# RWKV inverse on compact 64x64 blocks in quarters of TensorE's array, fold products alternating over the heads

## Chip, cores, metric

The kernel runs on one core of a Trainium2 chip. The metric is the device time of one execution in microseconds; of several executions the median is taken. Engines are named as in the profile: PE is TensorE, PEld its weight loads, DVE VectorE, ACT ScalarE, POOL GpSimd, SP the engine that issues most DMAs.

## What is computed

Two blocks of a language model, in float32, on 512 tokens of 1024 channels. The first block mixes the tokens with eight heads of forgetting attention and eight heads of an RWKV-7 recurrence, projects the result, and ends with a gated feed-forward layer. The second has an HGRN2 and a retention mixer and a retrieval over 16384 experts. The change lies in the RWKV recurrence alone. Cut to that, the reference is:

```python
def rwkv7_scan(r, w, k, v, a, b):
    """S_t = S diag(w_t) + (S a_t) b_t^T + v_t k_t^T ;  y_t = S_t r_t."""
    def step(S, inp):
        r_t, w_t, k_t, v_t, a_t, b_t = inp
        Sa = jnp.einsum('bhij,bhj->bhi', S, a_t)
        S = S * w_t[:, :, None, :] + Sa[..., None] * b_t[:, :, None, :] + v_t[..., None] * k_t[:, :, None, :]
        return S, jnp.einsum('bhij,bhj->bhi', S, r_t)
```

## The kernel before

The whole program is one list of instructions per engine. The kernel writes them in a loose order, and a scheduler at build time fixes the order on each engine; the engines then run their lists strictly in order and wait for each other by semaphores. So a change of a few instructions also moves their neighbours.

The recurrence is done in chunks of 64 tokens. Two heads share the 128 partitions: the even head lies on partitions 0 to 63, the odd one on 64 to 127. There are four such pairs of heads (c = 0 to 3), each with eight chunks, which are worked on in two groups of four: eight groups u in all. Within a chunk the 64 steps are turned into products, for which the inverse of I - N is needed, N a strictly triangular 64x64 matrix of each head and chunk.

For each pair of heads `rwkv_elem` (L655) makes decay, keys and gates of 512 tokens: long operations on VectorE and ScalarE. For each group then:

- `rwkv_group` (L721) makes the operands: scaled keys and queries (bh, BK, AR), the score products `ge` (L767: K = 64 rows, one head's half of the array, one bank a head), and masks them into NT (N of four chunks, L772), GM and AR. In NT each chunk has 128x128 elements with the two heads' blocks on the diagonal and zeros elsewhere (a memset, L738).
- `rwkv_inv` (L791) doubles the inverse, for two chunks at a time; two such halves h = 0, 1 alternate, with a bank pair each (i0 in A, i1 in B). It starts from the identity with the first level masked in (Tt, L808 and L809), transposed to T (L807 and L812). For each of five levels it makes NT^T T (L804 into PSUM, copied to Y by ScalarE, L818), Tt^T Y (L804, masked into T by VectorE, L821), and, but for the last level, the transpose of T (L807), copied to Tt by ScalarE (L825). All products are 128x128 by 128x128; both heads are in one product, since the matrices are block-diagonal.
- `rwkv_fold` (L829) multiplies the inverse with GM (`wg`, L836, copied to GS by ScalarE, L838), then with AT (`wf`, L843, K = 64, four products of one head and then four of the other, each head into bank C, which has one buffer), and VectorE adds each result to M (L844).
- `rwkv_scan` (L846) goes through the four chunks in sequence: a product of state and values (`ys`, L862), whose result is copied back into SV by VectorE and ScalarE (L865, L866) before the next; then it normalises (L871 to L891).

The driver interleaves them as software stages: for each u it prepares group u + 2, inverts group u + 1, folds and scans group u (L1582 to L1586). Banks are given by a string, `RB = "acc ge wg; A i0; B i1; C pe gv wf ys; D gt ga lt"`, with two buffers each for acc, A and B, one each for C and D. Behind the stage comes the output projection: its first half, over the attention's results, does not depend on the recurrence and is placed by the scheduler into gaps of TensorE's list from 440 us on; all later parts follow it.

The inverse in the code, cut:

```python
# rwkv_inv, B = [128, 2, 128]
def product(out, a, b):
    nc.tensor.matmul(out, a, b, start=True, stop=True)
...
for m in (2, 4, 8, 16, 32):
    py = self.b(f"i{h}", B)
    each(product, py, nt, tf)
    y = self.S(B, name=f"Y{h}")
    nc.scalar.activation(y, py, AF.Copy)
    px = self.b(f"i{h}", B)
    each(product, px, tt, y)
    nc.vector.copy_predicated(tf, mask(self.lv, self.levT[m]), px)
```

Of the kernel before, what the change touches and what calls it, by code (L numbers as in the profile page):

```python
# [12 lines left out]
U32 = mybir.dt.uint32  # L13
AF = mybir.ActivationFunctionType
ALU = mybir.AluOpType
AX = mybir.AxisListType

T = 512
# [5 lines left out]
# ---------------------------------------------------------------- host layout  # L24
def fm_tiles(w, cols=None):
    """[K, N] -> one [128, (K/128)*128] block per 128 output columns, split into ring tiles of 1024."""
    w = w if cols is None else w[:, cols]
    k, n = w.shape
    a = w.reshape(k // 128, 128, n // 128, 128).transpose(2, 1, 0, 3)
    return a.reshape(n // 128, 128, k // 1024, 1024).transpose(0, 2, 1, 3).reshape(-1, 128, 1024)  # L30


def tm_tiles(w):
    """[K, N] -> ring tiles of [128, 2 k-chunks, 512 columns], column blocks outermost."""
    k, n = w.shape
    a = w.reshape(k // 256, 2, 128, n // 512, 512).transpose(3, 0, 2, 1, 4)
    return a.reshape(-1, 128, 1024)


def fmvec(v):  # L40
# [4 lines left out]
NDENSE = 3      # token tiles whose experts are all computed; the last tile gathers its experts' rows  # L45
NFIFO = 40
IN_ORDER = ((0, 0), (0, 1), (0, 2), (0, 3), (1, 0), (1, 1), (1, 2), (1, 3))      # projections: mixer, heads
ONEHOT = "DDPDDDPP"     # engine of the second one-hot, by quartet of a block
NEARLY, NLATE, NLAG = 25, 3, 10      # products with expert_u before and after the gate matrix
# [3 lines left out]
    [x for n in range(8) for x in [(1, n), (0, n + GATE_AHEAD)] if x[1] < 8]    # gate a, branch; block  # L53
ATTN_STEP = 2
ELEM_AT = 2
FB = "acc; A m fpt; B fs; C pe fpo0; D fpo1"      # banks of the mixers' products
RB = "acc ge wg; A i0; B i1; C pe gv wf ys; D gt ga lt"
# [3 lines left out]
def shape_consts():  # L61
# [12 lines left out]
    us = [lev(m) for m in (2, 4, 8, 16, 32)] + [lev(m).T for m in (1, 2, 4, 8, 16, 32, 64)]  # L74
    out["cu"] = np.concatenate(us, 1).astype(np.uint32)
    scm = np.ones((128, T), np.float32)
# [13 lines left out]
def prep(inp):  # L90
    """Lays the inputs out; every array is a permutation, slice or stack of inputs, or depends on shapes alone."""
# [77 lines left out]
# ---------------------------------------------------------------- program  # L169
class Prog:  # L170
# [14 lines left out]
    # storage: every name of a tile stands for a tag with its number of buffers in the pool of the phase  # L185
    def open(self, es, name, spec, right=True, psum=False):
        """spec: "tag buffers name name ...; ..." """
# [9 lines left out]
    def banks(self, spec):  # L197
        """spec: "bank name name; ..." """
# [24 lines left out]
    # ring of weight tiles  # L223
# [36 lines left out]
    # products  # L260
    def mm3(self, out, a, b, start, stop):
        """out += a^T b with a, b given as exact (hi, lo) parts"""
# [5 lines left out]
    def gemm_fm(self, X, M=128, bank="acc", parts=1):  # L268
        """one block of 128 output features x 512 tokens; X: list of (hi, lo) FM chunks"""
# [12 lines left out]
    def gemm_tm(self, X, banks=("A", "A", "B", "B"), done=None, tail=2, head=1, ps=None, stop=True, hold=0):  # L282
        """512 output columns x 4 token tiles; the tiles end one after the other,
        the end of a tile behind the norm of the one `hold` before it"""
# [27 lines left out]
    def split(self, src, name):  # L312
        """FM f32 chunk in SBUF -> exact parts"""
# [8 lines left out]
    # constants  # L322
    def consts(self):
# [8 lines left out]
        ld(self.cu, I["cu"].rearrange("p (m n) -> p m n", n=128)[:, 5:12])  # L332
# [4 lines left out]
        # derived per-channel vectors  # L337
# [13 lines left out]
        # lower bound: softmax over the two rows, first row  # L351
# [8 lines left out]
        # f = lb + (1 - lb) (tanh / 2 + 1/2) = tanh * c1 + c0  # L360
# [7 lines left out]
    def attn_consts(self):  # L368
        """constants of the first mixers only"""
# [7 lines left out]
        self.lv = self.b("lv", [128, 5, 128], U32)  # L377
        ld(self.lv, I["cu"].rearrange("p (m n) -> p m n", n=128)[:, 0:5])
# [9 lines left out]
    def first_loads(self):  # L388
        """tokens, the first gain and the first weights in the order of their use"""
# [29 lines left out]
    def rstd_of(self, ss, n, eps, w=1):  # L419
        """(ss / n + eps) ** -0.5 of a small tile"""  # L420
# [7 lines left out]
    def new_U(self):  # L428
        """8 FM chunks of exact parts"""
# [4 lines left out]
    def rstd_row(self, ss):  # L434
        """(sum + eps) ** -0.5 of the two scaled square sums of a row"""
# [6 lines left out]
    def square(self, x, ss):  # L442
        """sum of squares / D along the row"""
# [3 lines left out]
    def norm_tile(self, i, gb, banks=("C", "D"), ss=None):  # L447
        """rmsnorm of one token tile of self.X, into its columns of the FM chunks; ss: with its first square sum"""
# [24 lines left out]
    def norm_fm(self, gb):  # L473
        """rmsnorm of self.X as 8 FM chunks of exact parts"""
# [6 lines left out]
    def tm_norm(self, X, gp, gn, early=None):  # L481
        """self.X += rmsnorm(X^T w) * gp, and the FM chunks of rmsnorm(self.X) * gn;
        early: the two halves of the product begun with the first chunks"""
# [35 lines left out]
    # ------------------------------------------------------------ block 1  # L519
# [10 lines left out]
    def lat_part(self, U):  # L530
# [19 lines left out]
        # forget gates of the attention heads: rows 32..39  # L550
# [18 lines left out]
    def fox_proj(self, c, U):  # L569
        """queries, keys and values of two heads"""  # L570
# [84 lines left out]
    def rwkv_elem(self, c):  # L655
        """two heads of the RWKV group on 128 channels"""
# [5 lines left out]
        # decay  # L662
# [15 lines left out]
        # in-context rate  # L678
# [9 lines left out]
        # normalised key  # L688
# [16 lines left out]
        # gate and bonus  # L705
# [15 lines left out]
    def rwkv_group(self, c, g_, e):  # L721
        """operands of four chunks: with Z = [state; values] of a head and U = (I - N)^-1 A0^T Z,
        y = A1^T Z + B1^T U and the next state is D^T Z + Bu^T U"""
# [8 lines left out]
        ar = self.b("AR", [128, 4, 2, 2, 64])         # chunk, A0 or A1, head, token  # L732
# [938 lines left out]
```

## Time and profile before

| | us |
|---|---|
| median of 3 runs | 3137.03 |
| lowest, highest | 3127.26, 3152.71 |
| span of the profiled execution, first to last instruction | 3129.2 |

The page gives the span alone; the time of that execution beside it is not listed. A run's time takes in what lies around the span.

How to read the profile: the busy time of an engine is the union of its records. A matmul's record is modelled and includes the way through the array, so the next one starts before it ends, and gaps shorter than a record do not show. A float32 product appears as two records, each with a weight load, since it is done in two passes; a transpose as one. Shapes are written as rows of the array x columns of weights, then rows x moving columns, so `64*128 64x128` is a product that uses half of the rows. "Chain" is the sequence of work that ended last, followed back from the end.

### The profile page before, as it was taken

What the parts mean: (1) busy time and instruction counts of PE and PEld (TensorE: products, weight loads), DVE (VectorE), ACT (ScalarE), POOL (GpSimd) and SP (SyncE); (2) the same over time, 40 slices, a digit from 0 to 9 for tenths busy, and PEclk for the clock granted to TensorE, in tenths of its full rate; (3) what the DMA queues carried; (4) which work ended last, traced back from release to release, by engine and by line L of the source; (5) the groups of instructions that cost most, each with busy time, mean ns of one, the idle gap of its engine ahead of it and who ended that gap; (6) DMA issues with size and microseconds to landing.
All of it is one profiled execution on the core that took longest, in us unless ns stands there. A gap on an engine that the chain in (4) does not pass through costs nothing.

```text
span 3129.2 us, 40869 instructions
## 1 busy us (share of the span) xinstructions
PE 2961.4 (95%) x15129; PEld 2547.7 (81%) x15129; DVE 1938.7 (62%) x3421; ACT 1228.4 (39%) x1925; POOL 1508.5 (48%) x1150
## 2 busy tenths in 40 slices
PE   7999898999999999999999978888999999999998
PEld 6877787888878878888888868887888888888876
DVE  4247755443135653555423899997777777787788
ACT  5455644222243433444423324565333333333333
POOL 3222213222245652333323457866767677667665
PEclk9998999999999999999999989999999999999999
DMA  4120013333332213222333223446888988888886
GB/s 156 56 68 8 1 38 109 97 98 97 95 113 69 62 47 101 85 85 85 90 116 123 92 68 95 142 169 219 297 275 293 308 289 298 299 280 299 285 310 240
DMA packets 174359, 473.65 MB, mean 151 GB/s; under 512 B 15056, under 2 KB 64592, under 8 KB 172624
## 3 DMA queue, kind: packets, MB, share of 16 engines
q1 hardware_dynamic: 137296, 336.80, 33.8%
q0 software_dynamic: 36864, 134.23, 12.2%
q8 instruction: 120, 1.97, 0.3%
q14 instruction: 79, 0.65, 0.1%
HBM read 439.49 MB, written 31.46 MB: 151 GB/s over the span
## 4 chain that ended last, share of the span: by engine, by line
PE 69%; DVE 15%; DMA 7%; issue 5%; ACT 2%; POOL 1%; SPq 0%; DVEq 0%; POOLq 0%; ACTq 0%
PE acc L266 13%; PE acc L265 13%; PE acc L264 13%; DMA urow<-ev,ei 3%; PE A L266 3%; PE A L264 3%; PE A L265 3%; PE B L266 3%; PE B L265 3%; PE B L264 3%; DMA urow<-eu,ei 2%; PE pg L1377 2%; DVE lo L241 2%; PE i L804 1%; PE lev L981 1%
## 5 line engine op out<-in xcount | busy, mean ns | idle before, releaser
L241 POOL TENSOR_TENSOR lo<-raw,hi 128x1024 fp32r<-128x1024 f32 x278 | 689.6, 2481 | 912.9 <-ACT hi L238 875.8
L238 ACT ACTIVATE hi<-raw 128x1024 fp32r<-128x1024 f32 x501 | 529.3, 1057 | 1065.7 <-PE acc L265 441.4
L266 PE MATMUL acc<-u,lo 128*128 128x512 f32 (+3 forms) x2344 | 864.6, 369 | 39.2 <-DVE lo L241 21.2
L264 PE MATMUL acc<-u,hi 128*128 128x512 f32 (+3 forms) x2344 | 862.4, 369 | 15.0 <-ACT x L1392 6.3
L265 PE MATMUL acc<-u,hi 128*128 128x512 f32 (+3 forms) x2344 | 862.1, 368 | 0.7 <-DVE u L471 0.7
L266 PEld LDWEIGHTS acc<-u,lo 128*128 128x128 f32 (+1 forms) x2344 | 448.1, 191 | 96.2 <-DVE lo L241 27.6
L264 PEld LDWEIGHTS acc<-u,hi 128*128 128x128 f32 (+1 forms) x2344 | 447.8, 191 | 70.0 <-ACT eact L1392 6.7
L265 PEld LDWEIGHTS acc<-u,hi 128*128 128x128 f32 (+1 forms) x2344 | 448.3, 191 | 54.8 <-issue 2.7
L241 DVE TENSOR_TENSOR lo<-raw,hi 128x1024 fp32r<-128x1024 f32 x223 | 304.4, 1365 | 301.1 <-ACT hi L238 299.9
L1332 DVE SCALAR_TENSOR_TENSOR urow<-urow,h4row 128x1024 f32<-128x1024 f32 x128 | 201.5, 1595 | 109.2 <-DMA urow<-eu,ei 108.9
L1342 DVE SCALAR_TENSOR_TENSOR po<-urow,act,po 128x1024 f32<-128x1024 f32 x127 | 203.2, 1600 | 84.9 <-DMA urow<-ev,ei 83.5
L1324 POOL DMA_INDIRECT urow<-eu,ei x128 | 193.5, 1512 | 32.6 <-issue 19.0
L1324 POOL DMA_INDIRECT urow<-ev,ei x128 | 176.6, 1380 | 37.8 <-issue 18.2
L1403 ACT ACTIVATE wh<-wf 128x384 fp32r<-128x384 f32 x128 | 67.1, 525 | 272.3 <-PE D L265 243.5
L1368 DVE TENSOR_SCALAR ohA<-iota,slT 128x128 f32<-128x128 f32 x384 | 129.8, 404 | 0.9 <-PE pg L1377 0.7
L1377 PE MATMUL pg<-ohB,ohA 128*128 128x128 f32 x768 | 106.3, 280 | 25.0 <-DVE ohB L1374 12.5
L1377 PEld LDWEIGHTS pg<-ohB,ohA 128*128 128x128 f32 x768 | 97.4, 191 | 32.7 <-ACT gstage L1379 16.1
L1379 ACT ACTIVATE gstage<-pg 128x512 f32<-128x512 f32 x96 | 99.5, 1089 | 57.8 <-PE pg L1377 57.7
L1372 POOL TENSOR_SCALAR ohB<-iota,slT 128x128 f32<-128x128 f32 x144 | 98.2, 698 | 39.9 <-PE pg L1377 39.7
L266 PE MATMUL A<-hi,wl 128*128 128x512 f32 x256 | 95.8, 399 | 10.0 <-DVE wl L1404 9.9
L265 PE MATMUL A<-lo,wh 128*128 128x512 f32 x256 | 101.0, 395 | 0.8 <-POOL lo L241 0.8
L264 PE MATMUL A<-hi,wh 128*128 128x512 f32 x256 | 99.8, 390 | 0.6 <-ACT wh L1403 0.6
(539 smaller groups left out, 5395.9 us busy)
## 6 DMA issues: line engine op xcount, KB each, us to landing
raw<-ut SPq DMA_DIRECT2D x128, 512.0 KB
raw<-ev SPq DMA_DIRECT2D x128, 512.0 KB
raw<-w_ret SPq DMA_DIRECT2D x48, 512.0 KB
gd<-gstage SPq DMA_DIRECT2D x12, 2048.0 KB
gread<-gd SPq DMA_DIRECT2D x32, 768.0 KB
raw<-w_gu SPq DMA_DIRECT2D x44, 512.0 KB
raw<-w_hg SPq DMA_DIRECT2D x32, 512.0 KB
raw<-w_in SPq DMA_DIRECT2D x27, 512.0 KB
```

The lines of the kernel that those rows point to most:

```text
L238: self.nc.scalar.activation(hi, raw, AF.Copy)
L241: r = eng.tensor_tensor(lo, raw, hi.bitcast(F32), op=ALU.subtract)
L264: mm(out, a[0], b[0], start=start, stop=False)
L265: mm(out, a[0], b[1], start=False, stop=False)
L266: return mm(out, a[1], b[0], start=False, stop=stop).ins
L1324: r = nc.gpsimd.indirect_dma_start(out=u, out_offset=None, in_=src, in_offset=bass.IndirectOffsetOnAxis(ap=ei[:, s:s + 1], axis=0))
L1332: nc.vector.scalar_tensor_tensor(u, u, 1.0, row, op0=ALU.mult, op1=ALU.mult, accum_out=act[:, s:s + 1])
L1342: nc.vector.scalar_tensor_tensor(o, u, act[:, s:s + 1], o, op0=ALU.mult, op1=ALU.add)
L1368: nc.vector.tensor_scalar(A4[:, r], self.iota, sl[:, 0, k + r:k + r + 1], sl[:, 2, k + r:k + r + 1], op0=ALU.is_equal, op1=ALU.mult)
L1372: nc.gpsimd.tensor_scalar(B4[:, r], self.iota, sl[:, 1, k + r:k + r + 1], None, op0=ALU.is_equal)
L1377: last = nc.tensor.matmul(p[:, r, :], A4[:, r], B4[:, r], start=True, stop=True)
L1379: nc.scalar.activation(st[:, :, q * 4:q * 4 + 4].rearrange("p j t -> p t j"), p, AF.Copy)
```

## The change

The inverse keeps only the two heads' own 64x64 blocks, side by side on the partitions. NT, T, Tt and Y have 64 columns a chunk instead of 128, the memset of NT goes, and the masks become a table of their own (`cl`). A product of 128x128 becomes two of 64x64, on the upper left and on the lower right quarter of the array, and the transposes become plain products with a 64x64 identity (`ic`). The first product of the fold becomes two quarters as well; the second alternates over the heads, both results being held at once in the two buffers of acc. Line numbers of the new file are 1 to 6 away from those of the old one.

```diff
-RB = "acc ge wg; A i0; B i1; C pe gv wf ys; D gt ga lt"
+RB = "acc ge wg wf; A i0; B i1; C pe gv ys; D gt ga lt"
...
-    us = [lev(m) for m in (2, 4, 8, 16, 32)] + [lev(m).T for m in (1, 2, 4, 8, 16, 32, 64)]
+    us = [lev(m).T for m in (1, 2, 4, 8, 16, 32, 64)]
     out["cu"] = np.concatenate(us, 1).astype(np.uint32)
+    own = lambda a: np.concatenate([a[:64, :64], a[64:, 64:]], 0)
+    out["cl"] = np.concatenate([own(lev(m)) for m in (2, 4, 8, 16, 32)] + [own(lev(1).T)], 1).astype(np.uint32)
...
-        self.lv = self.b("lv", [128, 5, 128], U32)
+        self.lv = self.b("lv", [128, 6, 64], U32)
...
-        nt = self.S([128, 4, 128], name="NT")
+        nt = self.S([128, 4, 64], name="NT")
...
-        nc.gpsimd.memset(nt, 0.0)
...
-            TT(nt[R, :, 64 * par:64 * par + 64], pe[par][R, :, 0, :], mk[R, None, 0].to_broadcast(B3), op=ALU.mult)
+            TT(nt[R], pe[par][R, :, 0, :], mk[R, None, 0].to_broadcast(B3), op=ALU.mult)
...
     def rwkv_inv(self, e, g_, h):
-        B = [128, 2, 128]
+        HV = (slice(0, 64), slice(64, 128))
+        B = [128, 2, 64]
...
         def product(out, a, b):
-            nc.tensor.matmul(out, a, b, start=True, stop=True)
+            for i in range(2):
+                for R in HV:
+                    nc.tensor.matmul(out[R, i], a[R, i], b[R, i], start=True, stop=True)
         def transpose(out, a):
-            nc.tensor.transpose(out, a, self.ident)
-        nc.gpsimd.tensor_copy(tt, self.ident[:, None, :].to_broadcast(B))
-        nc.vector.copy_predicated(tt, mask(self.cu, self.levTt[1]), nt)
+            for i in range(2):
+                for R in HV:
+                    nc.tensor.matmul(out[R, i], a[R, i], self.ic[R], start=True, stop=True)
+        nc.gpsimd.tensor_copy(tt, self.ic[:, None, :].to_broadcast(B))
+        nc.vector.copy_predicated(tt, mask(5), nt)
...
     def rwkv_fold(self, e, g_):
...
         for i in range(4):
-            nc.tensor.matmul(pg[:, i, :], G["tf", i // 2][:, i % 2], G["gm"][:, i].rearrange("p a b -> p (a b)"), start=True, stop=True)
+            for R in HV:
+                nc.tensor.matmul(pg[R, i, :], G["tf", i // 2][R, i % 2], G["gm"][R, i].rearrange("p a b -> p (a b)"),
+                                 start=True, stop=True)
...
-        for par in range(2):
-            R = HV[par]
-            pf = self.b("wf", [128, 4, 2, 64])
-            for i in range(4):
-                nc.tensor.matmul(pf[:, i], G["at"][R, i, :], gs[R, i, :], start=True, stop=True)
-            nc.vector.tensor_tensor(G["m1"][:, :, par], pf, G["m1"][:, :, par], op=ALU.add)
+        pf = [self.b("wf", [128, 4, 2, 64]) for _ in range(2)]
+        for i in range(4):
+            for par in range(2):
+                R = HV[par]
+                nc.tensor.matmul(pf[par][:, i], G["at"][R, i, :], gs[R, i, :], start=True, stop=True)
+        for par in range(2):
+            nc.vector.tensor_tensor(G["m1"][:, :, par], pf[par], G["m1"][:, :, par], op=ALU.add)
```

The scheduler's order moves with it. The first place is TensorE's list in the middle of the stage, where an inverse runs beside the scan of the group before it. Before (a row is line, operation, result <- moving, weights or the other way round, size of the result, count; `i` are the banks of the inverse):

```order
L862 MATMUL ys<-SV,M_2306 128x64 x2
L804 MATMUL i_3061<-Y_3059,Tt_2935 128x128 x2
L807 MATMUL i_3198<-ident,Tt_3194 128x128 x2
L836 MATMUL wg<-GM,T_2928 128x128 x2
L804 MATMUL i_3202<-T_3187,NT 128x128 x2
L862 MATMUL ys<-SV,M_2306 128x64 x2
L804 MATMUL i_3215<-T_3195,NT 128x128 x2
```

After, in the same kind of place (L805 and L810 are the products and the former transposes of the inverse, L868 is `ys`):

```order
L868 MATMUL ys<-SV,M_2686 128x64 x2
L805 MATMUL i_3516<-Y_3514,Tt_3442 64x64 x4
L805 MATMUL i_3535<-Y_3533,Tt_3432 64x64 x4
L868 MATMUL ys<-SV,M_2686 128x64 x2
L810 MATMUL i_3522<-ic,T_3443 64x64 x4
L805 MATMUL i_3547<-T_3443,NT 64x64 x4
L810 MATMUL i_3541<-ic,T_3433 64x64 x4
L805 MATMUL i_3566<-T_3433,NT 64x64 x4
```

Groups of two full products have become groups of four quarter products, and the scan's `ys`, which use all rows and columns, stand between them as before.

The second place is the second half of a fold, `wf`, on TensorE. Before, with the numbers of the tiles:

```order
L843 MATMUL wf_3072<-GS_3070,AT_2354 128x128 x4
L807 MATMUL i1_3017<-ident_83,T1_2936 128x128 x2
L804 MATMUL i1_3034<-T1_2936,NT_2567 128x128 x2
L804 MATMUL i0_3026<-Y0_3024,Tt0_2927 128x128 x2
L767 MATMUL ge_3155<-AR_3127,BK_3128 128x128 x4
L804 MATMUL i1_3039<-Y1_3037,Tt1_2935 128x128 x2
L767 MATMUL ge_3156<-AR_3127,BK_3128 128x128 x4
L843 MATMUL wf_3078<-GS_3070,AT_2354 128x128 x4
```

After:

```order
L848 MATMUL wf_3319<-GS_3317,AT_2411 128x128
L848 MATMUL wf_3320<-GS_3317,AT_2411 128x128
L848 MATMUL wf_3319<-GS_3317,AT_2411 128x128
L848 MATMUL wf_3320<-GS_3317,AT_2411 128x128
L848 MATMUL wf_3319<-GS_3317,AT_2411 128x128
L848 MATMUL wf_3320<-GS_3317,AT_2411 128x128
```

The two heads' products, which stood apart with other work between them, now alternate one by one, in two tiles that are held at the same time; in five of the eight folds other products still stand between some of them.

## Rows read from the trace of the kernel before

**Rows 1.** Head of the page and its part 1, TensorE.
```profile
span 3129.2 us, 40869 instructions
...
PE 2961.4 (95%) x15129; PEld 2547.7 (81%) x15129; DVE 1938.7 (62%) x3421; ACT 1228.4 (39%) x1925; POOL 1508.5 (48%) x1150
```

**Rows 2.** Busy time by stretch: from:to, length, each engine's busy time, PEclk, DMA.
```profile
240.00:276.00 36.00, 30.70 (x166) 21.37 (x166) 32.02 (x63) 24.13 (x56) 11.23 (x18) 0.81 0.05 15
276.00:312.00 36.00, 35.13 (x297) 33.34 (x296) 18.75 (x48) 20.61 (x61) 5.60 (x12) 1.00 0.00 1
312.00:340.00 28.00, 23.81 (x150) 17.20 (x149) 22.77 (x48) 19.32 (x45) 9.37 (x12) 1.00 0.00 1
340.00:371.00 31.00, 29.59 (x238) 26.90 (x238) 18.30 (x46) 19.18 (x55) 5.86 (x12) 1.00 0.01 2
371.00:404.00 33.00, 28.55 (x194) 22.08 (x193) 28.41 (x58) 19.72 (x46) 8.96 (x11) 1.00 0.00 1
404.00:440.00 36.00, 35.44 (x293) 33.28 (x293) 19.26 (x54) 24.33 (x71) 4.71 (x6) 1.00 0.01 2
```

**Rows 3.** Chain that ended last, shares by line, of the six stretches in turn.
```profile
by line: DVE bh L753 8.8%; DVE AR L774 7.2%; DVE T L821 7.1%; PE pe L664 5.8%; PE pe L680 5.6%; PE gt L756 5.3%; issue 4.9%; PE i L804 4.7%; DVE Tt L809 4.3%; PE pe L692 4.3%; DVE NT L772 4.2%; DVE BK L743 4.2%; PE i L807 3.8%; DVE AR L741 
by line: PE i L804 47.6%; PE i L807 11.8%; PE wf L843 11.2%; PE ys L862 8.8%; PE wg L836 5.5%; PE ge L767 5.4%; ACT yl L871 2.1%; ACT M L775 1.8%; PE gv L784 1.2%; PE gt L756 1.2%; PE ga L778 1.2%; issue 1.0%; ACT SV L866 0.6%; PE lt L887 0
by line: DVE bh L753 8.1%; DVE T L821 7.1%; DVE Tt L809 5.6%; PE i L804 5.5%; DVE BK L743 5.3%; DVE AR L774 4.9%; ACT L696 4.6%; ACT L697 4.6%; DVE BK L746 3.9%; PE pe L680 3.8%; DVE k L687 3.8%; PE pe L664 3.8%; issue 3.5%; DVE NT L772 2.7
by line: PE i L804 36.4%; PE wf L843 10.1%; PE i L807 9.4%; PE ys L862 9.3%; PE ge L767 7.1%; ACT SV L788 3.5%; PE pe L664 3.4%; issue 3.0%; PE wg L836 2.9%; ACT yl L871 2.5%; DVE bh L753 2.2%; PE ga L778 2.1%; ACT M L775 2.0%; ACT Y L818 1
by line: DVE T L821 8.5%; DVE AR L774 8.1%; DVE bh L753 7.2%; DVE Tt L809 6.8%; DVE AR L741 5.1%; DVE BK L743 4.5%; DVE NT L772 4.2%; issue 4.1%; ACT L696 3.9%; ACT L697 3.9%; DVE M L844 3.9%; POOL rb L425 3.8%; DVE BK L746 3.8%; DVE L L671
by line: PE i L804 41.9%; PE ys L862 15.4%; PE i L807 12.5%; PE wf L843 12.3%; PE wg L836 4.1%; ACT SV L788 2.4%; ACT mixa L641 1.7%; DVE M L844 1.6%; PE A L264 1.4%; issue 1.3%; DVE T L821 1.3%; PE acc L638 1.3%; PE gt L756 1.2%; PE ga L77
```

**Rows 4.** Groups by line and shape; L807 with Tt by its line.
```profile
L804 PE MATMUL i<-Y,Tt 128*128 128x128 f32 x320 | 50.4, 285 | 1.1 <-ACT Y L818 0.8
...
L804 PE MATMUL i<-T,NT 128*128 128x128 f32 x320 | 50.1, 280 | 0.0
...
L1005 DVE COPY_PREDICATED dg<-cu,lev 128x512 f32<-128x512 uint32 x48 | 35.2, 736 | 35.1 <-PE lev L981 30.7 <-POOL dg L988 4.3
...
L821 DVE COPY_PREDICATED T<-lv,i 128x256 f32<-128x256 uint32 x80 | 34.8, 441 | 15.9 <-PE i L804 15.2
...
L807 PE MATMUL i<-ident,T 128*128 128x128 f32 x128 | 25.9, 284 | 4.9 <-DVE T L821 4.6
...
L807 PE MATMUL i<-ident,Tt x32: 272/273/474, 246.4 to 420.3; 128*128 128x128 f32 x32
```

**Rows 5.** Timeline of TensorE at 415 us: start, us, engine, line, tiles, records.
```profile
415.12 0.61 PE L804 MATMUL i<-Y,Tt 128*128 128x128 f32 x4
415.65 1.16 PE L843 MATMUL wf<-GS,AT 64*128 64x128 f32 x8
416.74 0.71 PE L804 MATMUL i<-Y,Tt 128*128 128x128 f32 x4
417.29 0.38 PE L807 MATMUL i<-ident,Tt 128*128 128x128 f32 x2
```

**Rows 6.** Timeline at 981 us, eight full records and eight half-wide weight loads.
```profile
980.85 1.05 PE L981 MATMUL lev<-qp,hk 128*128 128x128 f32 x8
...
981.83 0.54 PEld L998 LDWEIGHTS lev<-qp,hk 128*64 128x64 f32 x8
```

**Rows 7.** Line L998, weight loads: min/median/max ns of one.
```profile
L998 PEld LDWEIGHTS lev<-qp,hk x64: 132/138/227, 981.8 to 1149.2; 128*64 128x64 f32 x64
```

**Rows 8.** Timeline of TensorE at 253 us and at 282 us.
```profile
253.69 1.71 PE L767 MATMUL ge<-AR,BK 64*128 64x128 f32 x16
...
282.34 0.27 PE L767 MATMUL ge<-AR,BK 64*128 64x128 f32 x1
282.35 0.27 PE L843 MATMUL wf<-GS,AT 64*128 64x128 f32 x1
```

More of the change, by code (lines that the diff above doesn't have):

```diff
@@ L331, in consts @@
         self.cu = cp.tile([128, 7, 128], U32, name="cu")
-        ld(self.cu, I["cu"].rearrange("p (m n) -> p m n", n=128)[:, 5:12])
+        ld(self.cu, I["cu"].rearrange("p (m n) -> p m n", n=128))
         self.levTt = {1: 0, 2: 1, 4: 2, 8: 3, 16: 4, 32: 5, 64: 6}
@@ L376, in attn_consts @@
         nc.vector.tensor_copy(self.causb, cf[:, 256:384])
-        self.lv = self.b("lv", [128, 5, 128], U32)
-        ld(self.lv, I["cu"].rearrange("p (m n) -> p m n", n=128)[:, 0:5])
+        self.lv = self.b("lv", [128, 6, 64], U32)
+        ld(self.lv, I["cl"].rearrange("p (m n) -> p m n", n=64))
         self.levT = {2: 0, 4: 1, 8: 2, 16: 3, 32: 4}
@@ L793, in rwkv_inv, with product @@
         nc = self.nc
-        B = [128, 2, 128]
+        HV = (slice(0, 64), slice(64, 128))
+        B = [128, 2, 64]
         nt = e["G", g_]["nt"][:, 2 * h:2 * h + 2]
         tt, tf = self.S(B, name=f"Tt{h}"), self.S(B, name=f"T{h}")
-        mask = lambda t_, i: t_[:, i, None, :].to_broadcast(B)
-        def each(op, out, *a):
+        mask = lambda i: self.lv[:, i, None, :].to_broadcast(B)
+        def product(out, a, b):
             for i in range(2):
-                op(out[:, i], *[x[:, i] for x in a])
-        def product(out, a, b):
-            nc.tensor.matmul(out, a, b, start=True, stop=True)
+                for R in HV:
+                    nc.tensor.matmul(out[R, i], a[R, i], b[R, i], start=True, stop=True)
         def transpose(out, a):
-            nc.tensor.transpose(out, a, self.ident)
-        nc.gpsimd.tensor_copy(tt, self.ident[:, None, :].to_broadcast(B))
-        nc.vector.copy_predicated(tt, mask(self.cu, self.levTt[1]), nt)
+            for i in range(2):
[3 more added lines that the diff above has]
+        nc.vector.copy_predicated(tt, mask(5), nt)
         pt = self.b(f"i{h}", B)
-        each(transpose, pt, tt)
+        transpose(pt, tt)
         nc.scalar.activation(tf, pt, AF.Copy)
@@ L815, in rwkv_inv @@
             py = self.b(f"i{h}", B)
-            each(product, py, nt, tf)
+            product(py, nt, tf)
             y = self.S(B, name=f"Y{h}")
@@ L819, in rwkv_inv @@
             px = self.b(f"i{h}", B)
-            each(product, px, tt, y)
-            nc.vector.copy_predicated(tf, mask(self.lv, self.levT[m]), px)
+            product(px, tt, y)
+            nc.vector.copy_predicated(tf, mask(self.levT[m]), px)
             if m < 32:
                 pt = self.b(f"i{h}", B)
-                each(transpose, pt, tf)
+                transpose(pt, tf)
                 nc.scalar.activation(tt, pt, AF.Copy)
```

## Prediction

> **What bounds the kernel now.** I read the page first: TensorE is busy for 95% of the span [rows 1]. But one 128-wide float32 record lasts 0.28 us while the next one starts 0.11 us after it (worked out below), so "busy" hides gaps. The change lies in the recurrent mixer alone, which runs from about 235 to 475 us; all the other work comes behind it in the order of each engine, so what this stage gains or loses moves the end by the same amount. I therefore cut the stage into six stretches [rows 2] and read the chain of each [rows 3]. Three stretches (276 to 312, 340 to 371, 404 to 440 us; 103 us in all) have 297, 238 and 293 TensorE records: 297 x 0.11 = 33 of 36 us, and the chain there is TensorE's own products, the inverse (L804, L807) above all. In the other three (97 us) the same engine has half as many records, VectorE is busy 32.0 of 36, 22.8 of 28 and 28.4 of 33 us, and the chain is the preparation of the operands on VectorE. So a change of TensorE's time counts in the first three, a change of VectorE's in the others.
>
> **What a product costs.** A float32 product is two records, a transpose one: the 160 products of each kind are 320 records, the 160 transposes 128 + 32 [rows 4]. Eight full records last 1.05 us, one 0.28, so a record every (1.05 - 0.28) / 7 = 0.11 us [rows 4, 6]. A group of the inverse (two chunks) so takes 4 x 0.11 = 0.44 us for a product and 0.22 us for a transpose.
>
> After the change a product group is four 64x64 products, 8 records; a transpose group too, since the transposes become products with the identity (2 records each instead of one). What one record costs has to be put together. The nearest row has 64 weight columns and 64 moving ones: its weight loads last 0.138 us and eight of them 0.54 [rows 6, 7], one every (0.54 - 0.138) / 7 = 0.058 us. One after the other, a quarter group is 8 x 0.058 = 0.46 us, no better than today's product and twice today's transpose. The change lives on whether the two quarters, upper-left and lower-right, run beside each other. Rows 8 speak for it: a score product of one half of the rows and a fold product of the other start at 282.34 and 282.35 us and both last 0.27 us as ever; and 16 score records, the two halves one behind the other, take 1.71 us where eight fold records of one half take 1.16 [rows 5, 8], eight more for 0.55 instead of 0.89. Side by side, a group is 0.232 us. Ends: 0.232 and 0.464; I take the lower, because those are 64-row parts of the same array with the same kind of record.
>
> There is a rule against it. In all of rows 8 the two partners write two different banks. The Trainium skill, TensorEngine Tiling (Array Packing), section Restrictions and Gotchas, says that different row tiles write to different PSUM banks and can't access one bank at the same time. The two quarters of a group write one bank, on different partitions; no row shows such a pair. By the rule a group stays at 0.464 us, which is my second rival; for the fold's two halves, with a bank each, rule and rows agree.
>
> **The sum, three stretches bound by TensorE.** From the shares of rows 3:
> - Products L804: 47.6% of 36 + 36.4% of 31 + 41.9% of 36 = 43.5 us, times 0.232 / 0.44: -20.6 us.
> - Transposes L807: 11.8%, 9.4%, 12.5% = 11.7 us, times 0.232 / 0.22: +0.6.
> - Fold, second half (wf): 11.2%, 10.1%, 12.3% = 11.6 us. Alternating halves would take off half, 5.8; other shapes stand between some of its products in the new order, so I take -4 (ends 0 and -5.8).
> - Fold, first half (wg): 16 records with 64 weight columns but 128 moving ones, two at a time: 16 x 0.11 / 2 = 0.88 us a group, as 8 x 0.11 today: 0 (end: +4.4, its 4.4 us of chain doubled).
> - Changes of shape. Where the products change from full to half rows the engine stops: 4, 8 and 4 records from 415.12 to 417.29 us take 2.17 us, 16 x 0.11 = 1.76, so 0.41 for two changes, 0.2 each [rows 5]. From the first ge to the last ys the order has 67 places today where neighbouring products differ in shape (full, half rows), and 201 afterwards (full, half, quarter): 134 more. The inverse has 55 of its 800 x 0.11 = 88 us in these stretches, 63%: 84 changes, 84 x 0.2 = +16.8. Ends: 0, if the engine would wait for data at those places anyway, and 134 x 0.2 = +27.
>
> Together -7.2 us.
>
> **The other three stretches.** The masked copies of the inverse (L821 T, L809 Tt) are 11.4% of 36, 12.7% of 28 and 15.3% of 33 us of the chain [rows 3], 12.7 us. They shrink from 256 to 128 elements: 512 take 736 ns and 256 take 441 [rows 4], so 1.15 ns an element and 294 ns after: a third less, -4.2 us. The inverse's products on the chain there (8.5% and 5.5% of the first two, little in the third, some 5 us) shrink like the others, -2. The 50 further changes of shape fall where TensorE has slack (23.8 busy of 28 us); I count +1 (ends 0 and +10). Together -5.
>
> **What I count at nothing.** ScalarE's copies of Y, T and Tt halve as well; it is busy 20.6 of 36 us, never the bound (0 to -3). The memset of NT on GpSimd goes: busy 5.6 of 36 us, hidden. The mask table is smaller by 128 KB at the start: under 1 us. The fold's result moves from bank C to the two acc buffers: its two halves now wait for both, which ge and wg use too, and behind a waiting fold product stand the next products of the inverse on the same in-order queue. Cover: the scheduler's order keeps two or three inverse groups ahead of it. Without cover, eight folds that wait out one score group of 1.71 us [rows 8] are +14; with bank C free for ys, some microseconds less. I take 0. Behind 440 us the last folds give another -1.
>
> **Total.** -7.2 - 5 - 1 = -13 us. Against the profiled span of 3129.2 us [rows 1] that is 3116; the page gives no other time of that execution, and the median of the runs, 3137.0, lies 7.8 us over the span, so I predict 3124 us. A per cent is 31 us, about what a measurement of this kernel can tell from no change.
>
> **Rivals.**
> 1. *The changes of shape cost nothing visible, and the order tightens* (chance 0.2). TensorE would wait for VectorE at those places anyway, now that its products are short: -20.6 + 0.6 - 5.8 - 7 = -33, 3104 us. For it: after the change no engine is near its limit in these stretches. Against: rows 5 have no waiting next to the change, only the stop.
> 2. *The quarters take turns* (0.15; the bank rule). Products 43.5 x 0.464 / 0.44: +2.4; transposes 11.7 x 0.464 / 0.22: +13; wg +4.4; fold -4, since it has two banks; changes +16.8; other stretches -4 + 1: +29 in all, 3166 us. It decides from the point where a pair's second member starts 0.1 us or more behind the first instead of some nanoseconds. For it: no row has a pair in one bank. Against: rows 8, and different partitions.
> 3. *No visible effect* (0.1): the recurrence from chunk to chunk and the chain of ten copies per inverse set the pace of the TensorE stretches as soon as its products are short: 3137 us.
> 4. *A lower clock* (0.03): in the first stretch, where TensorE waits most, the granted clock was 0.81, against 1.00 later [rows 2]. At 0.81 the 103 us become 127: +24 - 13, 3148 us.
>
> **Chances and range.** The forecast itself has 0.52, with a range of its own of 3108 to 3140. Faster by over 1% (under 3106): rival 1 mostly and the tail of the forecast, 0.19. Slower by over 1% (over 3168): half of rival 2 and a fold that waits, 0.11. Within 1%: 0.7. The range reaches from rival 1 with its last 10 us (ScalarE and free banks) to rival 2's near side: 3094 to 3160.
>
> **What would show it.** Right: pairs of quarter records that start within some nanoseconds; a product group that follows its neighbour after 0.23 us; T copies of about 0.29 us; the last ys some 13 us earlier in the span; more stops of 0.2 us. Wrong: groups of 0.46 us; TensorE's stretches no shorter though the records are; PEclk under 1 between 276 and 440 us; a fold that waits for ge's readers; the gain given back in the products of the output projection behind 440 us, which fill TensorE's gaps at the end of the stage.

## The result, and the profile after

The changed kernel takes 3146.57 us (median), the kernel before 3133.18 us in the same comparison: a ratio of 1.0055, 95% interval 1.0037 to 1.0073. So it is 13 us slower by the medians and 17 by the ratio, where 13 faster was forecast; by the bound of a per cent it is "no change", and 3146.57 lies in the range. The sign is wrong, and that needs a cause.

The profiled execution of after spans 3138.3 us, 9.1 more than before. The head of its page and TensorE's line [rows 1]:

```profile
span 3138.3 us, 43221 instructions
...
PE 2956.9 (94%) x16313; PEld 2528.9 (81%) x16313; DVE 1929.0 (61%) x3421; ACT 1207.7 (38%) x1925; POOL 1503.1 (48%) x1142
```

The first thing to look at is whether the quarters run side by side. Groups by line and shape, after (count | busy us, mean ns of one | idle before, releaser) [rows 4]:

```profile
L805 PE MATMUL i<-Y,Tt 64*64 64x64 f32 x640 | 36.2, 238 | 6.9 <-ACT Y L821 6.7
L805 PE MATMUL i<-T,NT 64*64 64x64 f32 x640 | 35.6, 234 | 0.1
L810 PE MATMUL i<-ic,T 64*64 64x64 f32 x512 | 29.2, 237 | 6.0 <-DVE T L824 5.8
...
L824 DVE COPY_PREDICATED T<-lv,i 128x128 f32<-128x128 uint32 x80 | 22.9, 296 | 22.4 <-PE i L805 21.6
```

TensorE's timeline of after at 444 us [rows 5]:

```profile
444.67 0.40 PE L805 MATMUL i<-T,NT 64*64 64x64 f32 x8
444.91 0.40 PE L805 MATMUL i<-Y,Tt 64*64 64x64 f32 x8
445.24 0.66 PE L868 MATMUL ys<-SV,M 128*128 128x64 f32 x4
445.82 0.45 PE L805 MATMUL i<-Y,Tt 64*64 64x64 f32 x8
446.11 0.40 PE L810 MATMUL i<-ic,T 64*64 64x64 f32 x8
```

And of before at 431 us, where `ys` stands between products of its own shape:

```profile
431.06 0.56 PE L862 MATMUL ys<-SV,M 128*128 128x64 f32 x4
431.45 0.39 PE L807 MATMUL i<-ident,T 128*128 128x128 f32 x2
```

A group of eight quarter records is followed by the next after 0.24 us, as forecast (0.232); one after the other they would need 0.46. Around the state product `ys` the stops are there too. From start to next start, the group ahead of `ys` takes 0.33 us instead of 0.24, `ys` 0.58 instead of 0.39, and the group behind it 0.29 instead of 0.24: 0.33 us for two changes of shape, some 0.17 each. A masked copy takes 296 ns, where 294 was forecast. TensorE waits longer for the copies: 6.7 us for Y where it was 0.8, 5.8 for T where it was 4.6.

So the pieces are as forecast, and the time is not. The stretches tell where it goes (from:to, length, busy of PE, PEld, DVE, ACT, POOL, then PEclk) [rows 2]:

```profile
240.00:276.00 36.00, 27.81 (x292) 17.47 (x290) 26.79 (x56) 21.16 (x54) 8.76 (x13) 0.78 0.05 15
276.00:312.00 36.00, 31.68 (x595) 27.02 (x590) 16.38 (x51) 17.54 (x64) 4.63 (x11) 1.00 0.01 2
312.00:340.00 28.00, 19.83 (x179) 12.36 (x178) 19.97 (x43) 14.18 (x36) 7.14 (x9) 0.77 0.01 1
340.00:371.00 31.00, 28.90 (x462) 23.67 (x460) 17.42 (x48) 15.27 (x54) 5.20 (x10) 0.99 0.01 2
371.00:404.00 33.00, 28.75 (x246) 17.95 (x244) 23.11 (x47) 15.93 (x39) 7.76 (x11) 0.64 0.01 1
404.00:440.00 36.00, 31.27 (x525) 26.52 (x524) 16.70 (x51) 16.83 (x59) 5.28 (x8) 0.95 0.01 2
```

PEclk is what to see. Before, it was 1.00 in five of the six stretches; now it is 0.77 and 0.64 in the two stretches beside the preparation, 312 to 340 and 371 to 404. From 375.0 to 398.9 us it is 0.50 throughout, so TensorE runs at 1.2 GHz instead of 2.4. Before and after over the whole stage:

```profile
236.00:476.00 240.00, 221.92 (x1517) 185.27 (x1516) 155.61 (x342) 138.24 (x351) 54.73 (x80) 0.96 0.07 20
```

```profile
236.00:476.00 240.00, 204.64 (x2639) 155.34 (x2638) 140.82 (x335) 116.99 (x349) 46.71 (x72) 0.87 0.04 14
```

With two levels, a mean of 0.96 over 240 us is 240 x 0.04 x 2 = 19 us at half clock, and 0.87 is 62: 43 us more. What they do to single instructions shows TensorE's timeline of before at 384 and 389 us, and then of after at 388 us:

```profile
384.18 1.10 PE L714 MATMUL pe<-rk,ac 128*128 128x512 f32 x2 [2.01 <-ACT g L710]
...
388.98 1.71 PE L767 MATMUL ge<-AR,BK 64*128 64x128 f32 x16
```

```profile
388.00 2.07 PE L716 MATMUL pe<-rk,ac 128*128 128x512 f32 x2
390.00 0.69 PE L805 MATMUL i<-Y,Tt 64*64 64x64 f32 x8
390.74 2.07 PE L768 MATMUL ge<-AR,BK 64*128 64x128 f32 x11
```

The preparation's product takes 2.07 instead of 1.10 us, eleven score records more than sixteen did before, and these stand on the chain. The chain of after by line, of 312 to 340 and of 371 to 404, begins with the scores, 3.4 us in each. Among the lines of before's two chains [rows 3] they don't appear; in the first that is in part a matter of where the stretch ends, since from 341 to 344 us they are on it with 2.2 us:

```profile
by line: PE ge L768 12.1%; ACT L698 4.6%; ACT L699 4.6%; DVE L L673 4.4%; PE i L810 3.8%; PE gt L757 3.7%; POOL rb L427 3.6%; PE i L805 3.0%; DVE BK L747 3.0%; DVE x L896 2.8%; DVE ta L687 2.7%; DVE AR L742 2.7%; DVE kk L706 2.5%; DVE tn L7
...
by line: PE ge L768 10.3%; DVE AR L742 6.1%; issue 5.8%; ACT L698 3.9%; ACT L699 3.9%; DVE BK L744 3.6%; PE wf L848 3.5%; DVE L L673 3.4%; DVE bh L754 3.4%; DVE k L689 3.3%; PE gt L757 3.2%; POOL rb L427 3.1%; DVE T L824 2.8%; DVE BK L747 2
```

How far the inverse gets meanwhile is read from its own records by stretch, before (800 in all), then after (1920):

```profile
312.00:340.00 28.00, 12.77 (x94) 1.00 0.00 1
340.00:371.00 31.00, 19.45 (x144) 1.00 0.01 2
371.00:404.00 33.00, 15.31 (x108) 1.00 0.00 1
```

```profile
312.00:340.00 28.00, 6.74 (x137) 0.77 0.01 1
340.00:371.00 31.00, 14.19 (x336) 0.99 0.01 2
371.00:404.00 33.00, 10.26 (x176) 0.64 0.01 1
```

Before, 94 / 800 = 12% of the inverse is done from 312 to 340 and 14% from 371 to 404; after, 7% and 9%. In the stretch between them, at full clock, it is 18% in both. The inverse so ends 13.4 us later (its last record starts at 452.8 instead of 439.3 us). The last `ys` starts 3.9 us later, at 472.2 instead of 468.3, and the products of the output projection, which follow the inverse on TensorE, begin at 458.6 instead of 439.6 us.

A mark behind the stage is the first activation (`th`) of the feed-forward layer, which needs all of the mixers' results. Its line (min/median/max ns, first to last start) in before, in after, and in two kernels of the experiments, the fold alone and full blocks in the groups 1, 3 and 5:

```profile
L904 ACT ACTIVATE th<-acc x22: 577/582/582, 517.7 to 744.0; 128x512 f32<-128x512 f32 x22
L910 ACT ACTIVATE th<-acc x22: 576/582/582, 530.1 to 756.3; 128x512 f32<-128x512 f32 x22
L905 ACT ACTIVATE th<-acc x22: 577/582/582, 512.6 to 738.8; 128x512 f32<-128x512 f32 x22
L930 ACT ACTIVATE th<-acc x22: 577/582/582, 516.9 to 743.1; 128x512 f32<-128x512 f32 x22
```

It starts 12.4 us later in after than in before. The ends of the spans don't follow this mark one to one: the last of the four kernels is 0.8 us ahead of before here and its span ends 7.1 us later (3136.3 us), though no code in between was changed. So the mark is used below beside the medians; it is of one execution of each kernel.

### The profile page after: what moved, and what is told of

Read it like the earlier page. It is cut to its first block, busy times and chain, and to the rows that moved or that the text cites. A ratio compares the mean times of both kernels' runs of the same rounds, so it can differ in the third digit from the quotient of the medians.

```text
span 3138.3 us, 43221 instructions
## 1 busy us (share of the span) xinstructions
PE 2956.9 (94%) x16313; PEld 2528.9 (81%) x16313; DVE 1929.0 (61%) x3421; ACT 1207.7 (38%) x1925; POOL 1503.1 (48%) x1142
## 4 chain that ended last, share of the span: by engine, by line
PE 63%; DVE 16%; DMA 10%; issue 6%; ACT 3%; POOL 2%; SPq 0%; POOLq 0%; DVEq 0%; ACTq 0%
PE acc L268 12%; PE acc L267 12%; PE acc L266 12%; DMA urow<-ev,ei 4%; DMA urow<-eu,ei 4%; PE A L268 2%; PE A L267 2%; PE A L266 2%; PE B L268 2%; PE B L267 2%; PE B L266 2%; PE pg L1383 2%; DMA raw<-ev 2%; DVE lo L243 1%; DVE ohA L1374 1%
## 5 line engine op out<-in xcount | busy, mean ns | idle before, releaser
L268 PEld LDWEIGHTS acc<-u,lo 128*128 128x128 f32 (+1 forms) x2344 | 448.1, 191 | 89.7 <-DVE lo L243 23.6
L243 DVE TENSOR_TENSOR lo<-raw,hi 128x1024 fp32r<-128x1024 f32 x223 | 297.6, 1335 | 302.7 <-ACT hi L240 302.3
L1338 DVE SCALAR_TENSOR_TENSOR urow<-urow,h4row 128x1024 f32<-128x1024 f32 x128 | 208.7, 1650 | 112.1 <-DMA urow<-eu,ei 111.9
```

Source lines behind the costliest of these rows:

```text
L243: r = eng.tensor_tensor(lo, raw, hi.bitcast(F32), op=ALU.subtract)
L268: return mm(out, a[1], b[0], start=False, stop=stop).ins
L1338: nc.vector.scalar_tensor_tensor(u, u, 1.0, row, op0=ALU.mult, op1=ALU.mult, accum_out=act[:, s:s + 1])
```

## The experiments

Three theories at first: *clock* (the half clock beside the preparation), *shape* (changes of shape eat the gain) and *fold* (the fold's results in the acc buffers hold up the scores); later *order* (the scheduler places fewer groups of the inverse there, whatever the clock).

**Quarters alone, fold alone.** The change taken apart. In the first, after with

```
-RB = "acc ge wg wf; A i0; B i1; C pe gv ys; D gt ga lt"
+RB = "acc ge wg; A i0; B i1; C pe gv wf ys; D gt ga lt"
```

and the second half of the fold as in before; the second is before with the reverse edit.

> The kernel after with the second half of the fold put back as it was (one head after the other, in bank C); the quarters stay. Three theories of the loss of some 15 us. Clock (the short products leave TensorE so little to do in the stretches that VectorE bounds that its clock is granted at half, and the inverse falls behind there): the loss stays, 10 to 20 us above the kernel before. Shape (each change of shape stops TensorE 0.2 us and eats the gain): the loss falls by a few changes per fold only, 8 to 15 us above. Fold (the fold's results in the acc buffers hold up the scores): no loss any more, 0 to 10 us under the kernel before.

> The kernel before with the alternating second half of the fold in the acc buffers alone; no quarters. Clock: within 5 us of the kernel before, since the fold is a small share of TensorE's work. Shape: 0 to 3 us faster. Fold: the whole loss, 12 to 20 us slower.

Quarters alone: 3154.78 us, ratio to before 1.0066 [1.0041, 1.0090], 19 us by the medians, as the clock theory expected. Fold alone: 3127.03 against 3135.7, ratio 0.9975 [0.9955, 0.9996]. The fold theory falls: the new fold is a gain of some 8 us (more than any of the three expected), and the quarters alone cost at least as much as the whole change. The ratios of these two overlap; in the traces the quarters alone start the feed-forward layer at 539.3 us, 9 later than after. The fold alone is faster than both kernels. The stage of each, quarters first:

```profile
236.00:476.00 240.00, 209.47 (x2606) 160.93 (x2604) 137.76 (x329) 114.39 (x343) 44.60 (x70) 0.83 0.04 13
```

```profile
236.00:476.00 240.00, 220.98 (x1533) 185.92 (x1534) 161.40 (x345) 139.58 (x354) 57.65 (x83) 0.95 0.08 23
```

The clock goes with the loss: 0.83 and 0.95.

**Quarters in part of the groups.** The preparation runs beside the inverses of the groups 1, 3 and 5. Each inverse can be told to use full blocks (the transposes, the memset of NT and the first product of the fold go with it):

```
+FULL = (1, 3, 5)        # the other kernel: (2, 4, 6, 7)
...
 for i in range(2):
+    if full:
+        nc.tensor.matmul(out[:, i], a[:, i], b[:, i], start=True, stop=True)
+    else:
         for R in HV:
             nc.tensor.matmul(out[R, i], a[R, i], b[R, i], start=True, stop=True)
```

> The kernel after, but the inverses of the groups 1, 3 and 5 of the eight (those that run beside the elementwise preparation, where VectorE bounds) on full 128x128 blocks as before; the other five in quarters. Clock: the granted clock beside the preparation is back near the one of the kernel before (0.95 or more over the whole stage) and the loss is gone, from 10 us faster than the kernel before to equal. Shape: three eighths of the added changes go, so 6 to 12 us slower than the kernel before. Fold: the loss stays, 12 to 20 us slower.

> The kernel after, but the inverses of the groups 2, 4, 6 and 7 on full blocks, those that run mostly where TensorE bounds; 0, 1, 3 and 5 in quarters. Clock: the half clock beside the preparation stays, as does most of the loss, 10 to 20 us slower than the kernel before. Shape: half of the added changes go, 3 to 9 us slower. Fold: the loss stays, 12 to 20 us slower.

Full in 1, 3, 5: 3138.93 us, 1.0012 [0.9997, 1.0026]. Full in 2, 4, 6, 7: 3156.75, 1.0067 [1.0047, 1.0087]. Both are what the clock theory expected, within some 4 us, and the clock over the stage is 0.94 and 0.88. The two were timed beside the same runs of before and are 18 us apart: what after loses against before goes with the quarters of the groups beside the preparation. But the quarters of the other groups are not free. Both kernels have the new fold, and against the fold alone (3127.03 us, same comparison) the one with full blocks in 1, 3, 5 is 12 us slower by the medians and 4.3 at the mark in the traces, at nearly the same clock (0.94 and 0.95). So the quarters of 0, 2, 4, 6 and 7 gained nothing. Shape doesn't fit as the cause of the difference between the two: the trace has 202 changes of shape between 230 and 500 us in after (68 in before), 176 in the kernel without the loss and 151 in the one with it. (The fold alone has 58, so changes of shape can be part of the 12 us.) The pair also gives a price. Between the transposes (`gt`) of the fifth and the sixth group, the order puts 30 groups of the inverse in both, 13 of them full in the first kernel and 17 in the second. Full in 1, 3, 5 (first), full in 2, 4, 6, 7 (second):

```profile
332.45:359.44 26.99, 24.27 (x295) 20.66 (x293) 19.05 (x49) 13.89 (x45) 4.91 (x8) 1.00 0.01 2
```

```profile
333.94:367.74 33.80, 31.03 (x278) 26.43 (x276) 19.54 (x49) 14.37 (x44) 5.19 (x9) 0.75 0.00 1
```

VectorE's and ScalarE's work is the same within 0.5 us, the clock 1.00 against 0.75, the time 27.0 against 33.8 us. That is 6.8 us for 33.8 x 0.25 x 2 = 16.9 us at half clock: 0.4 us lost for each, an estimate from one pair of stretches whose orders differ a little. The whole stage gives the same: after against full in 1, 3, 5 has 240 x (0.94 - 0.87) x 2 = 34 us more at half clock, and its mark is 13.2 us later.

The order theory falls by the same kernels: ahead of the seventh group's `gt` stand 176 groups of the inverse in before, 158 in after and 156 in the kernel with full blocks in 1, 3, 5, which has no loss. It gets there with as few groups at 384.84 us, after at 392.91. Fewer groups ahead cost nothing if the preparation comes earlier by as much.

**More work for TensorE.** Two ways to bring the clock back. In the groups 1, 3 and 5 of after, each quarter product twice, or one full product of the identity ahead of each product group:

```
+for _ in range(2 if more else 1):
     nc.tensor.matmul(out[R, i], a[R, i], b[R, i], start=True, stop=True)
```

```
+if more:
+    nc.tensor.matmul(out.rearrange("p a b -> p (a b)"), self.ident, self.ident, start=True, stop=True)
```

> The kernel after, but in the inverses of the groups 1, 3 and 5 each quarter product is issued twice, one behind the other (60 groups of products, 0.23 us each, 14 us more for TensorE, no more changes of shape and no other copy). The places of the loss are known by now (the quarters of 1, 3 and 5); two theories are left of how it comes about. Clock (TensorE has so little to do there that half the clock is granted): the added work brings the granted clock of the stage from 0.87 towards 0.95, and the time falls although work was added: 0 to 10 us above the kernel before, where the kernel after is 15 above. Order (the scheduler's order places fewer groups of the inverse there, whatever the clock): no gain, 15 to 30 us above the kernel before.

> The kernel after, but in the inverses of the groups 1, 3 and 5 a full 128x128 product of the identity with itself goes ahead of each group of quarter products, into the same tile, which they overwrite (60 of them, 0.22 us each, and up to 120 more changes of shape, 0.2 us each: at most 37 us more for TensorE). Clock: the granted clock of the stage rises towards 0.95, 0 to 12 us above the kernel before. Order: 15 to 45 us above it.

3158.78 us, 1.0078 [1.0052, 1.0104], and 3161.97, 1.0090 [1.0061, 1.0118]: 26 and 30 us above before. Both miss what the clock theory expected and lie in the ranges of the order theory. But the clock, which they were to raise, did not rise over the stage, 0.84 and 0.87, so they don't decide between the two; the kernels with full blocks do. With twice as many quarter products the clock was somewhat higher beside the preparation (0.80 from 312 to 340 us, 0.79 from 371 to 404, where after has 0.77 and 0.64) and lower elsewhere. With the few full ones it was 0.91 and 0.88 there, also lower elsewhere, and their 0.22 us and two changes of shape each stand on TensorE's path. The theory as first put, that TensorE has too little to do, was too simple: in after PE is busy 28.75 of 33 us where the clock is 0.64. The next pair changes only the size of the weights.

**The same work on the full array and on a quarter.** In after, two products that nobody reads ahead of each of the preparation's products:

```
 def rwkv_elem(self, c):
+    def fill():
+        for j in range(2 if c else 0):
+            d = self.b(f"i{j % 2}")
+            nc.tensor.matmul(d, self.ident, self.cs, start=True, stop=True)
+            # partner: d[0:64], self.ident[0:64, 0:64], self.cs[0:64]
...
+    fill()
     ps = self.b("pe")
```

> The kernel after, with two products that nobody reads, full 128x128 weights by 512 columns into a tile of the inverse, ahead of each of the five products of the preparation of the channel blocks 1 to 3 (30 products, about 1 us each at the full clock, 31 us more for TensorE, all of it beside the preparation and next to products of the same shape). It is a pair with the one with quarter fillers, which takes TensorE as long. Clock (the half clock beside the preparation is what costs the time): the granted clock from 312 to 404 us rises from 0.64 to 0.88 towards 0.95 or more; between 10 us faster than the kernel after and 10 slower, since the fillers also stand in the way, and 10 to 20 us faster than its partner. Not the clock: the two are equal but for some 60 changes of shape of the partner, at most 9 us, both 10 to 30 us slower than the kernel after.

> The partner of the one with full fillers: the same 30 products nobody reads, as long (512 columns) but with 64x64 weights, a quarter of the array, and a change of shape on either side. Clock: the granted clock beside the preparation stays under 0.85, and it is 10 to 20 us slower than its partner. Not the clock: at most 9 us slower than its partner, for the changes of shape.

Full fillers 3163.13 us, 1.0076 [1.0050, 1.0103]; quarter fillers 3187.37 us, 1.0150 [1.0120, 1.0179]: 24 us apart, the one with full fillers faster, which is more than changes of shape were given (9 us) and 4 more than the clock theory expected. Two stretches beside the preparation and the stage, full fillers first:

```profile
312.00:340.00 28.00, 26.82 (x311) 16.89 (x311) 12.88 (x31) 13.83 (x38) 7.38 (x12) 1.00 0.01 1
371.00:404.00 33.00, 30.34 (x363) 19.21 (x358) 15.60 (x39) 18.61 (x52) 9.37 (x15) 1.00 0.01 2
236.00:476.00 240.00, 213.05 (x2598) 152.02 (x2595) 131.81 (x321) 110.14 (x334) 43.99 (x70) 0.88 0.01 4
```

```profile
312.00:340.00 28.00, 27.02 (x236) 13.30 (x232) 14.65 (x33) 12.57 (x32) 6.62 (x11) 0.76 0.01 1
371.00:404.00 33.00, 29.71 (x441) 24.43 (x438) 14.10 (x43) 17.63 (x58) 6.39 (x12) 0.76 0.01 2
236.00:476.00 240.00, 216.59 (x2218) 139.92 (x2215) 121.58 (x289) 100.68 (x298) 39.99 (x66) 0.75 0.01 4
```

TensorE is as busy in both (26.8 and 27.0 of 28 us), on full weights at 1.00 and on quarter weights at 0.76. (Its records get longer at the lower clock, so equal busy time is less work.) The changes of shape can't be it: 217 with full fillers, 193 with quarter ones. The fillers themselves show the level (min/median/max ns of a record), full, then quarter:

```profile
L668 PE MATMUL i<-ac,ident x60: 592/592/697, 278.7 to 405.0; 128*128 128x512 f32 x60
```

```profile
L668 PE MATMUL i<-ac,ident x60: 589/1057/1112, 275.3 to 432.3; 64*64 64x512 f32 x60
```

The same 512 columns take 592 ns, or 1057 with a quarter of the array at half clock (589 in its shortest record). Up to 14 of the 24 us are this stretching of the fillers, whose records cover 30.1 and 43.8 us and which after doesn't have; the price of half a clock is therefore taken from the pair before. Full fillers are no remedy either. The two kernels were timed beside different runs of before: against after they lose 17 us by the medians and 7 by the ratios, and in the traces the feed-forward layer starts 20 us later (550.2), where the clock theory allowed 10. Beside the preparation the clock came back (0.94 from 312 to 404 us), but from 240 to 276 us it was 0.64, where after has 0.78, and from 340 to 371 us 0.83 for 0.99. Over the whole stage it is 0.88, no better than after's 0.87, and 30 us of fillers were added.

**The price of a change of shape.** In before, ahead of the product groups of 2, 4, 6 and 7, one product of the same operands on a quarter, or on the full array:

```
+if more:
+    product(py[0:64, 0, 0:64], nt[0:64, 0, 0:64], tf[0:64, 0, 0:64])   # control: py[:, 0], nt[:, 0], tf[:, 0]
 each(product, py, nt, tf)
```

> The kernel before, with one 64x64 quarter product ahead of each group of full products in the inverses of the groups 2, 4, 6 and 7, overwritten by it (80 of them, 0.116 us each, and 160 more changes of shape). If a change of shape costs 0.2 us, 80 x 0.52 = 41 us more for TensorE, of which the stretches that TensorE bounds show some two thirds: 20 to 41 us slower. If it costs nothing: 0 to 9 us slower.

> The control of the one with quarter dummies: the kernel before with one full 128x128 product in the same places (80 of them, 0.22 us each, no change of shape). 80 x 0.22 = 18 us more for TensorE, two thirds of it to be seen: 9 to 18 us slower. If a change of shape has a price, this one is the faster of the two by 11 to 25 us; if not, the slower.

3166.27 us, 1.0099 [1.0073, 1.0126], and 3151.39, 1.0067 [1.0039, 1.0094]; the clock over the stage is 0.96 in both. The intervals just overlap; by the medians the quarter is 14.9 us dearer, though its product is shorter (80 x 0.116 = 9.3 us against 80 x 0.22 = 17.6). The first lies where a price for a change puts it, the control 1 to 3 us above its range (18), and their distance in the range of 11 to 25; at the mark in the traces they are 14.3 us apart. That is 23 us for 221 - 66 = 155 more changes, some 0.15 us each. TensorE's timeline at 417 us with the quarter dummy, then at 412 us with the full one:

```profile
417.42 0.56 PE L867 MATMUL ys<-SV,M 128*128 128x64 f32 x4
417.91 0.97 PE L805 MATMUL i<-Y,Tt 64*64 64x64 f32 x6
418.71 0.61 PE L841 MATMUL wg<-GM,T 128*128 128x128 f32 x4
```

```profile
412.98 0.83 PE L805 MATMUL i<-T,NT 128*128 128x128 f32 x6
413.65 0.83 PE L805 MATMUL i<-Y,Tt 128*128 128x128 f32 x6
```

Two records of a quarter and four full ones take 0.80 us from start to next start, six full ones 0.67, though a quarter record at its place is shorter; and the `ys` ahead takes 0.49 instead of 0.39. With 0.12 us for the two quarter records and 0.45 for the four full ones that is 0.23 + 0.10 us for two changes, again 0.17 each.

## Why the prediction was wrong, step by step

- *Quarters side by side, 0.232 us a group*: right, 0.24. The two partners write one PSUM bank, on different partitions, and start 5 to 10 ns apart in the trace. The Trainium skill, TensorEngine Tiling (Array Packing), section Restrictions and Gotchas, says that different row tiles can't access one bank at the same time; for these quarters the measurement differs, and it decides. Rival 2 is out.
- *Masked copies of 294 ns*: right (296), but their -4.2 us did not show, since the chain of these stretches grew elsewhere.
- *Changes of shape*: right in kind; 0.15 to 0.17 us for the 0.2 put in, and from the first score to the last `ys` the 201 places that were counted.
- *Three stretches bound by TensorE, -7.2*: too large. From 276 to 312 us, at full clock in both, 471 of 1920 inverse records run (24.5%) where it was 189 of 800 (23.6%): about 1 us in 36. Of the -7.2, the inverse was to bring -20.6 + 0.6 + 16.8 = -3.2; the kernel with quarters only in 0, 2, 4, 6 and 7 lost 4 to 12 us against the fold alone instead. Besides the changes of shape, TensorE now waits there: it is busy 31.7 of 36 us instead of 35.1, and its waits for the copies of Y and T grew by 7 us over the stage. That is rival 3 in part. Which of these costs how much is not shown.
- *Other three stretches, -5*: this is the step that failed. It read "the inverse's products there shrink like the others, -2", as if less work on an engine with slack could only help. With the full blocks gone, the granted clock beside the preparation fell to 1.2 GHz (0.77 and 0.64 in the two stretches, 0.50 from 375.0 to 398.9 us), and instead of bringing 5 us these stretches cost some 13. The preparation's own products on the chain took twice as long, and the inverse made 7% and 9% of its way there instead of 12% and 14%.
- *Rival 4, a lower clock, chance 0.03*: the right mechanism, put into the wrong stretches. It took the clock of the first stretch as a sign of waiting and applied it where TensorE has the most to do. In [rows 2] the first stretch, 0.81, already showed that the clock falls beside the preparation; the two later ones kept 1.00 only with the full-block inverse in them, and that was what the change took out. The prediction did list PEclk under 1 between 276 and 440 us among the signs of being wrong, and it is this sign that came. That the time still lies in the stated range is luck: the range was made wide for other rivals.
- *Fold in the acc buffers, counted at nothing, and -4 with -1 behind 440 us for its products*: right, even low; the fold alone brings some 8 us by the medians and 5 at the mark.
- *What this stage gains or loses moves the end by the same amount*: not so in single executions. From the mark to the end, after is 3 us faster than before and the kernel with full blocks in 1, 3, 5 is 8 us slower, with no change of code there.

The sum with the measured terms, by the mark in the traces: the fold alone -5.1, the quarters of 0, 2, 4, 6 and 7 +4.3, the quarters of 1, 3 and 5 +13.2, together +12.4 us. By the medians of the runs the first two are -9 and +12, and by the ratios (1.0055 and 1.0012) the third is +13: together +17. The third agrees with the clock: 34 us more at half clock x 0.4 = 14. What the second consists of stays open; each kernel also has its own order of instructions.

## What to carry to other kernels

Before making an engine's instructions smaller in a stretch that another engine bounds, look at what that does to TensorE's clock: here products on a quarter of the array kept it busy and left it at 1.2 GHz, and then the few products on the chain cost twice as much. Where neighbours have different shapes, count 0.15 us for each change. Don't expect packing to pay because TensorE bounds: the kernel that keeps full products beside the elementwise work and packs the rest is still 12 us slower than the new fold without any packing. When a change consists of two parts, run each alone: here one was worth -0.25% and was hidden under the other.

## What the runs showed of the hardware that was not expected

Equal busy time of TensorE went with different clocks. In 28 us with 26.8 busy on full fillers the granted clock was 1.00, with 27.0 busy on quarter fillers 0.76, and in after TensorE was busy 22.5 of the 23.9 us that it spent at 0.50. Issuing each quarter product twice left the stage at 0.84, where it was 0.87. Only full and quarter weights were compared; nothing between them was run. At half clock this kernel, bound by VectorE and by waits as much as by TensorE, lost 0.4 us a microsecond. Two quarter products that write one PSUM bank on different partitions ran side by side, 5 to 10 ns apart.
